# The inverse of the 16x16 diagonal blocks in a DeltaNet layer: VectorE's instructions given to GpSimd

## The chip, the cores and the metric

The kernel runs on 1 core of a Trainium2 chip. The metric is the device time of one execution in microseconds (us). In the profile the engines are PE (TensorE matmul), PEld (TensorE's weight loads), DVE (VectorE), ACT (ScalarE), POOL (GpSimd) and SP (SyncE, whose queue issues the DMAs here).

## The reference, cut to what matters

One layer of a streaming encoder: an input projection of 2176 tokens feeds three head groups (band attention, a gated DeltaNet, an S5 state space model), whose outputs go through an output projection and a feed-forward network. The change is in the DeltaNet. It works on chunks of 64 tokens and solves a unit lower triangular system in each:

```python
a_low = jnp.where(strict, jnp.einsum('bhnid,bhnjd->bhnij', k_beta, k) * decay, 0.0)
rhs = jnp.concatenate([v * beta[..., None], k_beta * jnp.exp(gc)[..., None]], axis=-1)
sol = lax.linalg.triangular_solve(a_low + jnp.eye(CHUNK, dtype=jnp.float32), rhs,
                                  left_side=True, lower=True, unit_diagonal=True)
u, w = sol[..., :d_v], sol[..., d_v:]
...
def step(state, xs):
    q_c, k_c, u_c, w_c, qk_c, gt_c = xs
    v_new = u_c - jnp.einsum('bhcd,bhde->bhce', w_c, state)
    o_c = jnp.einsum('bhcd,bhde->bhce', q_c, state) + jnp.einsum('bhij,bhje->bhie', qk_c, v_new)
    state = state * gt_c[..., None, None] + jnp.einsum('bhcd,bhce->bhde', k_c, v_new)
    return state, o_c
```

## The kernel before, in words

The mix stage runs three streams at once. The input projection (`project1`, then `project2_all`) is the dense one: each product is three fp32r matmuls (`mm3`, L63 to L67), whose operands are split into a high part by ACT (L60) and a low part by DVE (L61). The DeltaNet (`deltanet`, L166) goes over the 17 tiles of 128 tokens, in the order 0, 2, ..., 10, 16, 12, 14 of pairs (tile 16, the running streams, alone). The S5 stream joins when `project1` has ended. `mix` (L131) and `merge` (L121) interleave the three by hand-set paces; the Tile planner then lays the instructions out on each engine's queue at build time, and each engine runs its queue in that order.

For a pair of tiles the DeltaNet does this:

- `b_pre` (L474): convolution and SiLU (ACT L510, DVE L512, ACT L514, DVE L515), the norms (DVE L532 and the small ones of `rsqrt`, L343 to L350), factors `F` (DVE L544 to L549), the scaled q and k (DVE `qkn` L572 and `kdec` L577, POOL `qdkb` L574 and `R` L575, POOL `DM` L570), their transposes on PE (L583, L587), the products (PE L601) and their decays (DVE L603). The matrix `at` goes to DRAM and its 16x16 diagonal blocks come back as `blk` (SP L605, L606), one block on each partition: 32 partitions for a tile, 64 for a pair.
- `b_inverse` (L612): the changed function, once for a pair, 9 times in all. `Ti` begins as the identity (L620). Then 15 steps of forward substitution, each one product `tp` (L625) and one subtraction in `Ti` (L627), of 15 to 64 elements for a partition, each needing the one before it; then a transposed copy (L628). SP writes the two halves of `Ti` to the diagonal of a zeroed matrix in DRAM (`tD`, L635) and loads it back as `TU` (L636).
- `b_solve` (L640) on PE, DVE and ACT: products with `T` and `U` out of `TU` (PE L649), subtractions (DVE L661).
- `b_rec` (L674): the recurrence over the two chunks of a tile (PE L686 to L694, DVE L687 and L699, ACT L702), and `b_out` (L762): POOL `osq` L770, DVE L772, L775, L788, PE L786.

GpSimd has in this stage 7 instructions for a tile of the DeltaNet or less (L570, L574, L575, L608, L770, a few copies and memsets) and, from 600 us on, S5's products `tz` and `tw` (L957, L961). `Ti` has one buffer and `tp` too; `blk` has two, `TU` three.

Of the kernel before, what the change touches and what calls it, by code (L numbers as in the profile page):

```python
# [14 lines left out]
OP = mybir.AluOpType  # L15
# [26 lines left out]
class K:  # L42
# [292 lines left out]
    def rsqrt(self, pool, x, n, tag):  # L335

        V = self.nc.vector
        t = pool.tile([128, n], I32, name=tag + "t", tag=tag + "t")
# [3 lines left out]
        z = pool.tile([128, n], F32, name=tag + "z", tag=tag + "z")  # L342
        V.tensor_scalar(t, x.bitcast(I32), 1, None, OP.logical_shift_right)  # L343
        V.tensor_scalar(y, t, -1.0, float(0x5f3759df), OP.mult, OP.add)
        V.tensor_scalar(xh, x, -0.5, None, OP.mult)
        cur = y.bitcast(F32)
        for _ in range(3):
            V.tensor_tensor(s, cur, cur, OP.mult)
            V.tensor_tensor(s, s, xh, OP.mult)
            V.scalar_tensor_tensor(z, s, 1.5, cur, OP.add, OP.mult)  # L350
# [261 lines left out]
    def b_inverse(self, st, blk):  # L612

        nc = self.nc
        V = nc.vector
        bw = self.bw
        P = len(st) * 32
        Ti = bw.tile([P, 2, 16, 16], F32, name="Ti", tag="Ti", bufs=1)
        tp = bw.tile([P, 256], F32, name="tp", tag="tp")
        V.tensor_copy(Ti[:, 0], self.id16[:P])  # L620
        for j in range(15):
            m = 15 - j
            sh = [P, m, j + 1]
            pr = tp[:, :m * (j + 1)].rearrange("p (a b) -> p a b", a=m)
            V.tensor_tensor(pr, blk[:, j, j + 1:16].unsqueeze(2).to_broadcast(sh),  # L625
                            Ti[:, 0, j:j + 1, 0:j + 1].to_broadcast(sh), OP.mult)
            V.tensor_tensor(Ti[:, 0, j + 1:16, 0:j + 1], Ti[:, 0, j + 1:16, 0:j + 1], pr, OP.subtract)  # L627
        V.tensor_copy(Ti[:, 1], Ti[:, 0].rearrange("p i j -> p j i"))  # L628

        def load():  # L630
            for i, s in enumerate(st):
                k = s["t"] % NDIAG
                TU = bw.tile([128, 2, 4, 128], F32, name="TU", tag="TU", bufs=3)
                for u in range(2):
                    nc.sync.dma_start(self.diag_ap(self.tD[u, k]), Ti[i * 32:(i + 1) * 32, u])  # L635
                    nc.sync.dma_start(TU[:, u], self.heads_ap(self.tD[u, k]))  # L636
                yield TU[:, 0], TU[:, 1]
        return load
# [1296 lines left out]
```

## Time and profile before

| | before |
|---|---|
| median of 3 runs | 2851.4 us (2848.71 to 2852.71) |
| the profiled execution's own time | 2849.91 us |
| its span, first to last instruction | 2848.1 us |
| busy: PE, DVE, ACT, POOL | 2738.6, 1945.4, 1305.6, 1032.7 us |
| mean granted TensorE clock | 0.991 |

A row of the trace has the line of the kernel, the engine, what is written and read (`out<-in`, by the program's names) and the shape. Durations are in ns where a row gives min/median/max, otherwise in us. A wait row names who waited, for whom, the total in us, how many times, and the longest one. An engine's idle time matters where that engine sets the time.

### The profile page before, as it was taken

Reading aid. Unit: us, or ns where it says so; the run is one execution under the profiler, and the core shown is the slowest. Engines: PE = TensorE matmul, PEld = TensorE weight load, DVE = VectorE, ACT = ScalarE, POOL = GpSimd, SP = SyncE. Lnnn points to the kernel's source line nnn. Section 1 sums busy time; section 2 is a strip of 40 time slices with the busy share of each in tenths; the row PEclk is TensorE's granted clock in tenths of the full one; section 3 lists DMA queues with packets and bytes.
Section 4 is the critical chain, followed back from the end, with each engine's and each line's share of the span. In section 5 each row is a group of like instructions: output and inputs, shape, how many; then the busy total and the mean of one; then the engine's idle time right before and its main releaser. Section 6 shows DMA issues by size and latency. Waiting matters only on the chain.

```text
span 2848.1 us, 46357 instructions
## 1 busy us (share of the span) xinstructions
PE 2738.6 (96%) x16685; PEld 2405.1 (84%) x16685; DVE 1945.4 (68%) x4949; ACT 1305.6 (46%) x2714; POOL 1032.7 (36%) x914
## 2 busy tenths in 40 slices
PE   8999999989989899999999999999999999999998
PEld 8988888867677677788898998989989988999997
DVE  7587888788653788879855555576556557576766
ACT  3554554343355778612243443355334435444443
POOL 0010111232221232013354445345544453666664
PEclk9999999989999999999999999999999999999999
DMA  5644445555447652145631221153222214432321
GB/s 185 204 111 120 111 114 125 150 147 155 146 138 247 213 167 61 55 169 198 224 124 60 74 75 59 60 196 131 88 74 86 93 67 148 163 98 95 119 96 46
DMA packets 293436, 355.55 MB, mean 125 GB/s; under 512 B 85698, under 2 KB 218646, under 8 KB 292886
## 3 DMA queue, kind: packets, MB, share of 16 engines
q1 hardware_dynamic: 293206, 352.59, 39.4%
q8 instruction: 131, 2.15, 0.3%
q14 instruction: 99, 0.81, 0.1%
HBM read 280.25 MB, written 74.89 MB: 125 GB/s over the span
## 4 chain that ended last, share of the span: by engine, by line
PE 68%; DVE 16%; DMA 6%; issue 4%; ACT 3%; POOL 2%; SPq 1%; DVEq 0%; ACTq 0%; POOLq 0%
PE fdp L66 8%; PE fdp L65 8%; PE fdp L67 8%; PE pps L66 2%; PE pps L67 2%; PE pps L65 2%; PE fupz L67 2%; PE fupv L67 2%; PE fupv L65 2%; PE fupv L66 2%; PE fupz L65 2%; PE fupz L66 2%; PE fupx L65 2%; PE fupx L67 2%; PE fupx L66 2%
## 5 line engine op out<-in xcount | busy, mean ns | idle before, releaser
L1570 POOL TENSOR_TENSOR wu<-wur,wu 128x512 fp32r<-128x512 f32 x308 | 416.7, 1357 | 528.1 <-ACT wu L1569 527.4
L1696 DVE TENSOR_TENSOR fy<-fy,fdp 128x512 f32<-128x512 f32 x500 | 340.9, 685 | 255.8 <-PE fdp L67 255.5
L65 PE MATMUL fdp<-wdh,hh 128*128 128x512 f32 x1020 | 397.8, 390 | 1.2 <-DVE fy L1696 1.1
L66 PE MATMUL fdp<-wdl,hh 128*128 128x512 f32 x1020 | 397.3, 390 | 0.1
L67 PE MATMUL fdp<-wdh,hl 128*128 128x512 f32 x1020 | 397.1, 389 | 0.0
L1569 ACT CAST wu<-wur 128x512 fp32r<-128x512 f32 x308 | 189.6, 617 | 414.1 <-DMA wur<-in_w_upL 168.6
L65 PE MATMUL pps<-xh,wh 128*128 128x384 f32 (+2 forms) x800 | 279.6, 351 | 10.5 <-ACT xh L60 9.5
L66 PE MATMUL pps<-xl,wh 128*128 128x384 f32 (+2 forms) x800 | 279.3, 349 | 2.4 <-DVE xl L61 2.3
L67 PE MATMUL pps<-xh,wl 128*128 128x384 f32 (+2 forms) x800 | 277.1, 347 | 0.7 <-DVE wl L61 0.7
L65 PEld LDWEIGHTS fdp<-wdh,hh 128*128 128x128 f32 x1020 | 191.4, 188 | 41.0 <-DVE fy L1696 2.9
L67 PEld LDWEIGHTS fdp<-wdh,hl 128*128 128x128 f32 x1020 | 191.5, 188 | 40.0
L66 PEld LDWEIGHTS fdp<-wdl,hh 128*128 128x128 f32 x1020 | 191.5, 188 | 38.5 <-DVE wdl L61 0.7
L1643 DVE TENSOR_TENSOR hl<-fre,hh 128x384 fp32r<-128x384 f32 (+1 forms) x180 | 143.4, 797 | 85.1 <-ACT hh L1642 84.4
L60 ACT CAST wdh<-wdr 128x1024 fp32r<-128x1024 f32 x94 | 98.8, 1051 | 205.6 <-PE fdp L67 205.2
L65 PEld LDWEIGHTS pps<-xh,wh 128*128 128x128 f32 x800 | 151.9, 190 | 23.3 <-ACT xh L60 11.3
L61 DVE TENSOR_TENSOR wl<-wr,wh 128x512 fp32r<-128x512 f32 (+1 forms) x152 | 107.5, 716 | 86.3 <-ACT wh L60 84.2
L66 PEld LDWEIGHTS pps<-xl,wh 128*128 128x128 f32 x800 | 151.8, 190 | 14.3 <-DVE xl L61 5.5
L67 PEld LDWEIGHTS pps<-xh,wl 128*128 128x128 f32 x800 | 151.5, 189 | 12.4 <-DVE wl L61 2.5
L61 DVE TENSOR_TENSOR wdl<-wdr,wdh 128x1024 fp32r<-128x1024 f32 x94 | 133.1, 1421 | 6.6 <-ACT wdh L60 6.6
L60 ACT CAST wh<-wr 128x512 fp32r<-128x512 f32 (+1 forms) x152 | 92.3, 618 | 79.9 <-DMA wr<-in_w_inA 41.4
L1638 ACT ACTIVATE fre<-fre,ld_b_up 128x384 f32<-128x384 f32 (+1 forms) x144 | 85.9, 597 | 63.3 <-DVE fre L1647 40.3
L1229 ACT ACTIVATE P<-P,st 128x640 f32<-128x640 f32 (+4 forms) x128 | 97.2, 760 | 30.2 <-DVE st L1226 29.6
(569 smaller groups left out, 7241.7 us busy)
## 6 DMA issues: line engine op xcount, KB each, us to landing
wdr<-in_w_dnL SPq DMA_DIRECT2D x96, 512.0 KB
wur<-in_w_upL SPq DMA_DIRECT2D x88, 512.0 KB
wr<-in_w_inA SPq DMA_DIRECT2D x70, 512.0 KB
TU<-tD SPq DMA_DIRECT2D x34, 256.0 KB
y<-in_x SPq DMA_DIRECT2D x17, 512.0 KB
x<-y SPq DMA_DIRECT2D x17, 512.0 KB
fxr<-x SPq DMA_DIRECT2D x17, 512.0 KB
fy<-x SPq DMA_DIRECT2D x17, 512.0 KB
```

The costliest lines, as they stand in the source:

```text
L60: nc.scalar.copy(hi, src)
L61: nc.vector.tensor_tensor(lo, src, hi.bitcast(F32), OP.subtract)
L65: mm(out, lh, rh, start=first, stop=False, **kw)
L66: mm(out, lh, rl, start=False, stop=False, **kw)
L67: mm(out, ll, rh, start=False, stop=last, **kw)
L1229: self.nc.scalar.activation(x, x, AF.Exp, scale=-1.0, bias=st[:, q:q + 1], accum_out=st[:, 2 + q:3 + q])
L1569: self.nc.scalar.copy(hi, src)
L1570: P.tensor_tensor(lo, src, hi.bitcast(F32), OP.subtract)
L1638: nc.scalar.activation(r, src, AF.Relu, bias=self.bu[:, c * 2 + i:c * 2 + i + 1])
L1643: V.tensor_tensor(hl, r, hh.bitcast(F32), OP.subtract)
L1696: V.tensor_tensor(y, y, ps[x], OP.add)
```

## The change

`b_inverse` issues its 32 instructions (the identity copy, 15 products, 15 subtractions, the transposed copy) on GpSimd in place of VectorE. Shapes, tiles, buffers and the DMAs behind them stay as they are. `b_inverse` runs 9 times, so 288 instructions change their engine.

```diff
     def b_inverse(self, st, blk):
 
         nc = self.nc
-        V = nc.vector
+        P_ = nc.gpsimd
         bw = self.bw
         P = len(st) * 32
         Ti = bw.tile([P, 2, 16, 16], F32, name="Ti", tag="Ti", bufs=1)
         tp = bw.tile([P, 256], F32, name="tp", tag="tp")
-        V.tensor_copy(Ti[:, 0], self.id16[:P])
+        P_.tensor_copy(Ti[:, 0], self.id16[:P])
         for j in range(15):
             m = 15 - j
             sh = [P, m, j + 1]
             pr = tp[:, :m * (j + 1)].rearrange("p (a b) -> p a b", a=m)
-            V.tensor_tensor(pr, blk[:, j, j + 1:16].unsqueeze(2).to_broadcast(sh),
+            P_.tensor_tensor(pr, blk[:, j, j + 1:16].unsqueeze(2).to_broadcast(sh),
                             Ti[:, 0, j:j + 1, 0:j + 1].to_broadcast(sh), OP.mult)
-            V.tensor_tensor(Ti[:, 0, j + 1:16, 0:j + 1], Ti[:, 0, j + 1:16, 0:j + 1], pr, OP.subtract)
-        V.tensor_copy(Ti[:, 1], Ti[:, 0].rearrange("p i j -> p j i"))
+            P_.tensor_tensor(Ti[:, 0, j + 1:16, 0:j + 1], Ti[:, 0, j + 1:16, 0:j + 1], pr, OP.subtract)
+        P_.tensor_copy(Ti[:, 1], Ti[:, 0].rearrange("p i j -> p j i"))
```

## Rows read from the trace of the kernel before

**Rows 1.** Busy time by stretch: us, PE, PEld, DVE, ACT, POOL busy, PEclk, DMA share, GB/s.
```profile
165.00:700.00 535.00, 507.00 (x3761) 439.08 (x3760) 441.63 (x1706) 243.46 (x613) 106.60 (x165) 0.98 0.47 128
...
600.00:640.00 40.00, 31.20 (x167) 24.18 (x167) 37.44 (x120) 18.72 (x42) 15.48 (x19) 0.80 0.69 194
```

**Rows 2.** Instructions on the projection's PSUM tile: duration min/median/max, first and last start.
```profile
L67 PE MATMUL pps<-xh,wl x800: 274/338/628, 9.7 to 919.4; 128*128 128x384 f32 x91, 128*128 128x512 f32 x38, 128*128 128x256 f32 x31
```

**Rows 3.** What PE waited for, 165 to 700 us: total, times, longest.
```profile
PE bps L535 <- DVE s L515: 5.2, 3, 4.3
PE bps L587 <- POOL qdkb L574: 4.0, 7, 2.0
...
PE bqs L649 <- DMA TU<-tD: 0.4, 1, 0.4
...
PE brs L690 <- DVE vn L687: 0.3, 1, 0.3
```

**Rows 4.** Instructions on the tile Ti: by line, then their busy time from 165 to 760 us.
```profile
L625 DVE TENSOR_TENSOR tp<-blk,Ti x135: 155/200/701, 165.2 to 698.3; 64x15 f32<-64x15 f32 x16, 64x28 f32<-64x28 f32 x16, 64x39 f32<-64x39 f32 x16, 64x48 f32<-64x48 f32 x16
...
L628 DVE COPY Ti<-Ti x9: 367/371/1228, 172.6 to 699.8; 64x256 f32<-64x256 f32 x8, 32x256 f32<-32x256 f32 x1
...
sum 595.00, DVE 65.67; mean DVE 9.38
```

**Rows 5.** VectorE in order of time: start us, us; first and last of two inverses.
```profile
165.17 0.17 DVE L625 TENSOR_TENSOR tp<-blk,Ti 64x15 f32<-64x15 f32 x1 [2.31 <-DMA blk<-aD]
...
172.63 0.37 DVE L628 COPY Ti<-Ti 64x256 f32<-64x256 f32 x1
...
477.32 0.17 DVE L625 TENSOR_TENSOR tp<-blk,Ti 64x15 f32<-64x15 f32 x1
...
495.43 0.38 DVE L628 COPY Ti<-Ti 64x256 f32<-64x256 f32 x1
```

**Rows 6.** GpSimd's instructions of lines L570 and L574: duration ns min/median/max.
```profile
L570 POOL TENSOR_TENSOR DM<-DT,ld_c_mtri x17: 723/737/1354, 142.7 to 629.1; 128x256 f32<-128x256 f32 x17
...
L574 POOL TENSOR_TENSOR qdkb<-qk,F x17: 1037/1432/2250, 140.1 to 667.8; 128x512 f32<-128x512 f32 x17
```

**Rows 7.** GpSimd in order of time, feed-forward stage: two instructions, the second needs the first.
```profile
2572.57 1.29 POOL L1576 TENSOR_TENSOR wur<-wur 128x512 f32<-128x512 f32 x1
2573.94 1.30 POOL L1577 TENSOR_TENSOR wur<-wur 128x512 f32<-128x512 f32 x1
```

**Rows 8.** VectorE, then GpSimd, in order of time, 184 to 187 us; GpSimd at 621 us.
```profile
184.23 0.15 DVE L549 TENSOR_TENSOR F<-F,b_kd 128x4 f32<-128x4 f32 x1
184.31 0.68 DVE L572 TENSOR_TENSOR qkn<-qk,F 128x512 f32<-128x512 f32 x1
184.91 1.00 DVE L548 TENSOR_TENSOR F<-F,b_egc 128x4 f32<-128x4 f32 x1
...
184.46 1.43 POOL L574 TENSOR_TENSOR qdkb<-qk,F 128x512 f32<-128x512 f32 x1 [14.48 <-ACT s L510]
...
621.51 2.48 POOL L575 TENSOR_TENSOR R<-qk,F 128x256 f32<-128x256 f32 x1 [1.45 <-DVE F L549]
```

**Rows 9.** VectorE's groups, 165 to 700 us: busy us, mean ns, idle before.
```profile
L512 DVE SCALAR_TENSOR_TENSOR s<-cin,ld_b_cw,s 128x128 f32<-128x128 f32 x234 | 80.2, 358 | 1.9 <-ACT s L510 1.4
L61 DVE TENSOR_TENSOR wl<-wr,wh 128x512 fp32r<-128x512 f32 (+1 forms) x71 | 49.6, 701 | 3.7 <-ACT wh L60 3.4
```

**Rows 10.** The chain that ended last, 170 to 190 us: start us, us.
```profile
174.63 3.22 DMA TU<-tD
177.90 1.10 PE bqs L649 x8
```

**Rows 11.** SP's and PE's instructions in order of time, around 500 us.
```profile
497.43 2.08 SPq L636 DMA_DIRECT2D TU<-tD  x4
...
502.65 1.00 PE L649 MATMUL bqs<-at,TU 128*128 128x64 f32 x8
```

**Rows 12.** What SP's queue waited for, 165 to 705 us: total, times, longest.
```profile
SPq L635 <- DVE Ti L627: 7.3, 3, 4.5
```

## The prediction

> **What bounds the kernel now.** I read the busy times by stretch first, to find where the changed instructions lie and which engine is full there. They lie between 165 and 700 us, and in those 535 us PE is busy for 507.0 and DVE for 441.6, or 83% [rows 1]. The projections' matmuls run until 919 us [rows 2], far past the last inverse, so PE is the filler and the bound: whatever happens to an inverse counts only as far as PE idles longer or less. PE's idle time in the stretch is 535 - 507 = 28 us. The list of PE's waits says who ended it: fourteen of its rows name DVE, from 5.2 us down to 0.3, and they add up to 19.5 us; one names POOL with 4.0; one, of 0.4 us, names the load of `TU`, the way by which an inverse reaches PE [rows 3]. From 600 to 640 us DVE is busy for 37.4 of 40 us, PE for 31.2, and the granted clock is 0.80 (so part of that time passes at 1.2 GHz instead of 2.4) after PE has idled for 4.3 us on DVE's L515 [rows 1, 3]. So the stage is bound by PE, and what holds PE up is mostly DVE.
>
> Second I read the inverse itself. Its 288 instructions keep DVE busy for 65.7 us in all [rows 4]. As a chain, the first takes from 165.17 to 173.00 us, 7.8 us; the sixth from 477.32 to 495.81, 18.5 us, since DVE does other work between its links [rows 5].
>
> **Part one: what DVE gets back.** 65.7 us of work leave it. Some comes back as waiting, because the two engines hold each other up. DVE's L548, 128x4, took 1.00 us, where its sister L549 took 0.15: it ended with POOL's L574, which itself took 1.43 us against 1.04 at best, having started just behind DVE's L572 [rows 6, 8]. And a POOL instruction of 128x256, for which 0.73 us is usual, took 2.48 us at 621 us while DVE was full [rows 6, 8]. The Trainium skill, "SBUF — State Buffer", section "Who interferes with whom", says of this that a VectorE instruction with two SBUF inputs and a GpSimd instruction that reads SBUF exclude each other, and the later one waits for the whole of the earlier; the trace agrees (1.00 us against 0.15), and by that rule the change moves work between two engines of which one often stands still.
>
> How much comes back: between nothing and the whole time that the chain executes on POOL, 76 us (9 x 8.5, below). The two groups of DVE that read two SBUF operands in the rows shown, L512 and L61 with `wl`, are 80.2 + 49.6 = 130 of the 441.6 - 65.7 = 376 us that stay [rows 1, 9]; with the smaller ones I call it half, so about 35 us. Net relief: 65.7 - 35, about 30 us, 7% of DVE's time in the stretch. PE's waits on DVE (19.5 us) should fall by more than 7%, as they gather where DVE is full; I take a third, **-7 us**. Bounds: 0, and -28 (all 19.5 us and the 8 us that a clock of 0.80 costs in 40 us).
>
> **Part two: the chain on POOL.** No row shows POOL with 64 partitions and 15 to 64 elements. Its nearest rows are 737 ns for 256 elements [rows 6] and 1290 ns for 512 [rows 7]: 2.16 ns an element on top of 184 ns. The 30 linked instructions have 2 x 680 = 1360 elements together, so 30 x 0.184 + 1360 x 0.00216 = 8.5 us of execution. A link costs 0.08 us between two dependent instructions (2572.57 + 1.29 to 2573.94) [rows 7], 2.4 us for 30. The transposed copy of 256 elements lies between DVE's 0.37 [rows 4] and the 0.74 of a POOL instruction of that size; I take 0.5. Undisturbed chain: 11.4 us. Below, if small instructions cost only their share of 0.737 us: 6.8. Above, if each cost as much as 256 elements: 25. The identity copy is no link; it runs ahead, and counts as cheap as now.
>
> On top comes the wait for DVE, once for each link: 0.01 us by L570 (median less minimum), 0.40 by L574, which DVE's L572 always meets [rows 6]. I take 0.15, as links become ready at any moment, like L570: 30 x 0.15 = 4.5 us. Chain with waits: about 16 us, against 8 to 18 on DVE. So the latency hardly changes; what changes is whether the fixed order of the queues expects it.
>
> That order puts PE's first product with `TU` close behind its landing: the load issued at 174.63 lands after 3.22 us, and PE starts at 177.90, with nothing in between [rows 10]. Around 500 us a load issued at 497.43 should land by some 500.8, and PE starts at 502.65, 1.8 us of slack [rows 11]. Mean slack: 1 us. If the planner counts the undisturbed chain, each inverse comes 4.5 - 1 = 3.5 us too late, 9 x 3.5 = 31 us. Behind PE's waiting product stand the projections' matmuls, which have to be late with it. But while PE stands, DVE and ACT run ahead and later waits shrink, so I take half: **+15 us**. Bounds: 0 (the planner expects the waits, or PE is late anyway) and 55 (twice the waits for each link, nothing made up: 9 x (9 - 1) = 72, less what PE regains from DVE).
>
> **Part three: the queues it is moved past.** On DVE the inverse no longer delays the norm, split and recurrence work, which is in part one. On POOL it stands before `qdkb`, `R`, `DM` and `osq`, for each tile. `qdkb` feeds PE's transposes, which waited 4.0 us for it, 7 times [rows 3]. One link lasts some 0.3 us, so a neatly woven queue adds little; a late chain adds its lateness. **+1 us**, bounds 0 and 9. The first link waits for the landing of `blk`, on POOL as it did on DVE (2.31 us at 165.17) [rows 5]; POOL's queue stands behind it, and POOL is busy for 106.6 of 535 us [rows 1], so little is lost. SP's write of `Ti` waited 7.3 us for DVE's last links, 3 times, up to 4.5 [rows 12]; with weight loads queued behind it, a late chain there costs as it did. The number and sizes of the DMAs stay, at no cost: they are issued by SP either way. Memory stays, too.
>
> **Sum.** -7 + 15 + 1 = +9 us on a span of 2848.1 us. The profiled execution took 2849.9 us, 1.8 more than its span, and lies 1.5 us under the median of the runs, so I carry +9 to the median: 2851.4 + 9 = **2860 us**. About 0.2%, 5.7 us, is what a measurement of this kernel tells from no change.
>
> **The rivals.**
>
> *DVE's relief wins (faster).* Mechanism: DVE is what PE waits for, 19.5 of 28 us, and the 600 to 640 us stretch loses clock besides [rows 1, 3]. If half of those waits (10 us) and half of the clock's price (4) go and late chains cost 2 us, it is 12 us faster: 2839. For it: on DVE the chain took up to 18.5 us, on POOL it may be shorter. Against: the half that comes back as waiting. It decides if chains on POOL stay under what the order allows, slack of 1 us included.
>
> *No change, within 4 us: 2851.* Both parts are small because PE is full for 95% of the stretch. The Trainium skill, "Perfetto Trace Analysis", section "Optimizing Scalar/DVE Operations", points this way: offloading between those two engines might not help, as they share a read port. No row here weighs the sum of that.
>
> *POOL is starved (much slower).* Each time a link ends, DVE's next instruction with two operands takes its turn first, 0.36 us for L512, 0.70 for L61 [rows 9], as the 2.48 us of L575 show in the extreme [rows 8]. With 0.4 us a link, 12 us an inverse, 11 beyond the slack; half made up, 9 x 5.5 = 50 us; with the relief gone too, less 10 that stalled DVE work would have cost: +40, 2891. Against: L570's median lies only 0.01 us over its minimum.
>
> That the change would not do what it says can be left out: the engine is named in each call.
>
> **How the numbers follow.** Forecast (late chains cost more than the relief, +2 to +18 us): 0.37. DVE's relief wins: 0.27. No change: 0.22. Starved: 0.14. A quarter of the forecast's case and little of the faster one's fall within 5.7 us: slower 0.37 x 0.75 + 0.14 = 0.42, same 0.22 + 0.09 + 0.01 = 0.32, faster 0.26. The range runs from 2837 (under the faster case's 2839) to 2888 (just short of the starved case), which leaves out about a tenth on either side. Signs are mixed, so the forecast's own range is 2853 to 2869.
>
> **What would show it.** Right: 288 instructions move; DVE's busy time from 165 to 700 us falls by 30 us or so, not 66, with L512 and L61 longer in the mean; a chain on POOL takes 14 to 18 us; PE's waits for `TU` grow from 0.4 us to 10 and more, those on DVE fall below 15. Wrong: chains of 11 to 12 us and PE's waits for `TU` still under 3 us (then faster or the same), or chains over 22 us (then starved). What would upset the whole sum is a new order of the queues that moves PE's idle time to somewhere the rows above don't show.

## The result, and the profile after

The changed kernel takes 2920.1 us (median of 4 runs, 2917.3 to 2923.4), the kernel before 2850.7 us beside it: 1.0249 times as long, 95% interval 1.0237 to 1.0262. That is 69 us slower, where 2860 us and a range of 2837 to 2888 had been forecast. The sign was right, the size was not.

Almost all of the loss lies in the mix stage. The last matmuls of the projection start at 990.8 us, 71 us later than before [rows 2]; the span grew by 73.5 us, from 2848.1 to 2921.6. In the busy times by stretch (us of the stretch, then PE, PEld, DVE, ACT, POOL busy, PEclk, DMA share, GB/s), the first row answers to [rows 1]; the second takes the stage to its end:

```profile
165.00:700.00 535.00, 470.48 (x3367) 412.29 (x3365) 357.91 (x1275) 226.07 (x575) 174.38 (x398) 0.92 0.42 113
...
165.00:991.00 826.00, 728.90 (x4819) 619.66 (x4818) 524.97 (x1685) 344.02 (x811) 241.74 (x498) 0.93 0.47 131
```

The same stretch of the kernel before, to the end of its projection:

```profile
165.00:919.70 754.70, 706.92 (x4816) 599.40 (x4815) 555.24 (x1972) 342.80 (x811) 148.56 (x211) 0.98 0.50 143
```

With the same matmuls (4816 and 4819 records), PE stands idle for 826.0 - 728.9 = 97.1 us in place of 47.8, and is busy for 728.9 us in place of 706.9. So 49 of the 71 us are idle time. The other 22 are longer matmuls, which go with the lower granted clock (0.93 for 0.98).

The instructions on the tile `Ti` (duration ns min/median/max, first and last start) answer to [rows 4], now on POOL:

```profile
L625 POOL TENSOR_TENSOR tp<-blk,Ti x135: 203/282/1192, 166.2 to 748.6; 64x15 f32<-64x15 f32 x16, 64x28 f32<-64x28 f32 x16, 64x39 f32<-64x39 f32 x16, 64x48 f32<-64x48 f32 x16
L627 POOL TENSOR_TENSOR Ti<-Ti,tp x135: 212/294/769, 166.5 to 748.9; 64x15 f32<-64x15 f32 x16, 64x28 f32<-64x28 f32 x16, 64x39 f32<-64x39 f32 x16, 64x48 f32<-64x48 f32 x16
...
L628 POOL COPY Ti<-Ti x9: 594/603/676, 178.4 to 749.2; 64x256 f32<-64x256 f32 x8, 32x256 f32<-32x256 f32 x1
```

From the first link to the end of the copy, the nine chains take 11.8 to 15.4 us, 13.6 in the mean; on DVE they took 7.8 to 22.9, 15.5 in the mean. So the chains did not get longer, and yet the work that needs them is late. What PE waited for (165 to 770 us: total, times, longest) answers to [rows 3]:

```profile
PE bqs L649 <- DMA TU<-tD: 28.2, 6, 7.6
PE s5p L1019 <- DMA Tm<-kS: 10.5, 1, 10.5
PE brs L786 <- DVE osq L775: 8.0, 7, 2.4
PE pps L65 <- ACT wh L60: 6.2, 1, 6.2
PE bps L587 <- POOL qdkb L574: 5.6, 7, 2.4
PE pps L67 <- DVE wl L61: 5.3, 1, 5.3
```

SP's queue over the same time, which answers to [rows 12]:

```profile
SPq L635 <- POOL Ti L627: 77.7, 9, 11.8
```

SP now comes to the write of `Ti` too early at every inverse, by 77.7 / 9 = 8.6 us; before, 3 times and by 4.5 us at most [rows 12]. So the planner's order has SP at the write some 5 us after the first link of a chain that takes 13.6. What duration the planner reckons with, no run shows. PE comes too early as well. Here is PE in order of time at the first inverse, with the idle time before an instruction in brackets:

```profile
175.72 0.33 PE L66 MATMUL pps<-xl,wh 128*128 128x384 f32 x1
183.69 1.97 PE L649 MATMUL bqs<-at,TU 128*128 128x64 f32 x8 [7.63 <-DMA TU<-tD]
```

PE has nothing left before its first product 9.9 us after the first link (175.72 + 0.33 - 166.2). Before, it arrived there 12.3 us after the link, waited 0.4 us for `TU` [rows 3] and started at 12.7 us (165.17 [rows 5] to 177.90 [rows 10]). Counted so for all nine inverses, PE arrives 16.4 us after the first link in the mean, where it was 22.0. The chain needs 13.6, and from its last copy to PE's product at least another 4.7 us pass (179.01 to 183.69). PE's order thus leaves the chain 5.2 us at the first inverse and 11.7 in the mean.

What it costs that SP stands is seen at the last inverse. SP in order of time:

```profile
737.68 0.42 SPq L210 DMA_DIRECT2D wr<-in_w_inA  x1
749.15 0.98 SPq L635 DMA_DIRECT2D tD<-Ti  x2
750.22 1.36 SPq L983 DMA_DIRECT2D Tm<-kS  x2
```

and PE, which needs that `Tm` for the S5 stream, not for the DeltaNet:

```profile
753.56 0.79 PE L1019 MATMUL s5p<-U,Tm 128*128 128x136 f32 x2 [10.53 <-DMA Tm<-kS]
```

From 738.1 to 749.15 us SP issued nothing; the load of `Tm` stood behind the write.

### The profile page after: what moved, and what is told of

It reads as the page before. It is cut to its first block, busy times and chain, and to the rows that moved or that the text cites. A ratio compares the mean times of both kernels' runs of the same rounds, so it can differ in the third digit from the quotient of the medians.

```text
span 2921.6 us, 46374 instructions
## 1 busy us (share of the span) xinstructions
PE 2760.6 (94%) x16685; PEld 2424.7 (83%) x16685; DVE 1913.3 (65%) x4661; ACT 1307.0 (45%) x2714; POOL 1128.8 (39%) x1202
## 4 chain that ended last, share of the span: by engine, by line
PE 67%; DVE 13%; DMA 7%; POOL 4%; issue 4%; ACT 3%; SPq 1%; DVEq 0%; ACTq 0%; POOLq 0%
PE fdp L66 8%; PE fdp L65 8%; PE fdp L67 8%; PE pps L67 3%; PE pps L66 3%; PE pps L65 3%; PE bqs L649 2%; PE fupv L65 2%; PE fupv L67 2%; PE fupv L66 2%; PE fupz L65 2%; PE fupz L67 2%; PE fupz L66 2%; PE fupx L65 2%; PE fupx L67 2%
## 5 line engine op out<-in xcount | busy, mean ns | idle before, releaser
L60 ACT CAST wh<-wr 128x512 fp32r<-128x512 f32 (+1 forms) x152 | 92.7, 619 | 97.1 <-PE pps L66 40.7
```

Source lines behind the costliest of these rows:

```text
L60: nc.scalar.copy(hi, src)
```

## The experiments

**Three theories.** Theory 1, the order: the queues of PE and SP are laid out for a chain much shorter than the real one, so both stand. Theory 2, the port: the chain on POOL and DVE's work hold each other up. Theory 3, POOL's queue: what stands behind the chain on POOL is late. Where the expectations speak of holding a queue, every instruction of the mix on the named engine is tied to its predecessor in a given list, by place in the queue alone, without a semaphore; the planner lays out the rest. All ratios are against the kernel before, run on the same chip.

**1. The change in the old order.** PE's and SP's queues as they stand in the kernel before.

```diff
+ORDER = {
+...
+}
+
+def hold_order(nc, tc):
+    byname = {i.name: i for i in nc.cur_bb.bb.instructions}
+...
     with tile.TileContext(nc) as tc:
         K(nc, tc, A).run()
+        hold_order(nc, tc)
```

> The changed kernel, with the instructions of TensorE's and SyncE's queues held, up to the end of the mix, in the order that they have in the kernel before (PE and SP alone; DVE, ACT and POOL are left to the planner). Theory 1 (the order: the planner counts the POOL chain some 8 us too short and moves the solves' products and the tD writes ahead, so PE and SP stand before they are ready): in the old order PE comes to the first product 12 to 33 us after the first link and the POOL chain with its DMAs needs about 18, so only the first two or three inverses are late, by 4 to 6 us each; against that stands DVE's relief: 2840 to 2865 us, PE's waits for TU under 15 us in all (28.2 in the changed kernel), SP's waits for the chain under 25 (77.7). Theory 2 (POOL's chain holds DVE and POOL at the shared port) and theory 3 (POOL's own queue is held up by the chain, and what waits behind it is late): the order is no matter, 2900 us or more.

2877.0 us, 1.0091 (1.0076 to 1.0106): 44 of the 69 us are gone, and 25 stay, more than theory 1 alone allows. PE's and SP's waits, 165 to 770 us, and DVE's on POOL:

```profile
PE pps L66 <- DVE xl L61: 10.8, 2, 10.6
PE bqs L649 <- DMA TU<-tD: 8.8, 3, 5.9
```

```profile
SPq L635 <- POOL Ti L627: 12.4, 2, 9.9
```

```profile
DVE WB L964 <- POOL tw L961: 13.5, 4, 8.9
DVE ms L772 <- POOL osq L770: 11.3, 11, 3.8
```

The time lies above theory 1's range and below the other theories'. The waits for `TU` and for `Ti` are small again, as expected. New is that DVE stands for POOL. POOL in order of time at the longest of these waits (a chain had begun at 628.0 us, and nothing but its links ran until `tw`):

```profile
639.47 0.23 POOL L625 TENSOR_TENSOR tp<-blk,Ti 64x28 f32<-64x28 f32 x1
639.66 0.63 POOL L961 TENSOR_TENSOR tw<-st,pis 128x256 f32<-128x256 f32 x1
640.26 0.23 POOL L627 TENSOR_TENSOR Ti<-Ti,tp 64x28 f32<-64x28 f32 x1
640.46 0.63 POOL L961 TENSOR_TENSOR tw<-st,pis 128x256 f32<-128x256 f32 x1
```

and DVE, which needs the second `tw`:

```profile
641.12 0.69 DVE L964 TENSOR_TENSOR WB<-WB,tw 128x512 f32<-128x512 f32 x1 [8.90 <-POOL tw L961]
```

PE's wait of 10.6 us for `xl` follows from it, as `xl` stands behind `WB` in DVE's queue. Since PE's order is the same in both kernels, one of its instructions can be set beside the other: PE falls back by 6.6 us up to the first product with `TU`, and by 9.5 us in one step at 645.5 us.

**2. The old kernel in the new order.** The reverse: the chain on DVE, PE and SP held as in the changed kernel. The edit is the one of experiment 1, on the kernel before, with the changed kernel's list.

> The kernel before, its chain on DVE, with TensorE's and SyncE's queues held in the order of the changed kernel. Theory 1: the loss comes with the order, without any POOL chain: PE stands at TU and SP at the tD write as in the changed kernel, 2880 to 2930 us, PE's waits for TU 20 us or more. Theories 2 and 3: nothing runs on POOL that did not before, 2845 to 2860 us.

2928.6 us, 1.0265 (1.0248 to 1.0282). With the inverse on DVE and nothing new on POOL, the order by itself costs 77 us. That is more than the change itself lost: on DVE the seventh and the eighth chain take 21.4 us each here, and PE stands 10.7 and 11.6 us for them. PE and SP wait in the places where they wait in the changed kernel, though the engine behind them is another:

```profile
PE bqs L649 <- DMA TU<-tD: 40.6, 8, 11.6
PE s5p L1019 <- DMA Tm<-kS: 11.2, 2, 10.6
PE brs L786 <- DVE osq L775: 6.9, 6, 1.5
PE pps L65 <- ACT wh L60: 6.1, 1, 6.1
```

```profile
SPq L635 <- DVE Ti L627: 53.9, 7, 13.7
```

**3. No chain, old order.** What DVE's relief is worth.

```diff
-        tp = bw.tile([P, 256], F32, name="tp", tag="tp")
-        P_.tensor_copy(Ti[:, 0], self.id16[:P])
-        for j in range(15):
-...
-        P_.tensor_copy(Ti[:, 1], Ti[:, 0].rearrange("p i j -> p j i"))
+        for u in range(2):
+            nc.vector.scalar_tensor_tensor(Ti[:, u], blk, 0.0, self.id16[:P], OP.mult, OP.add)
```

> The changed kernel without a chain at all (two DVE instructions write the unit matrix into Ti from blk, the inverse is left out), TensorE's and SyncE's queues in the order of the kernel before: what DVE's relief alone is worth in that order. Working of the prediction: 65.7 us off DVE are worth at most 28 us: 2823 to 2845 us. If 2848 to 2853, DVE's relief is worth nothing in that order and there was never anything to gain but by the order. Theories 2 and 3 say the same of this run as theory 1.

2850.2 us, 0.9993 (0.9984 to 1.0002): nothing. 18 instructions stand where 288 stood, and nothing is won. The first stretch [rows 1]:

```profile
165.00:700.00 535.00, 508.11 (x3777) 441.36 (x3776) 412.82 (x1446) 244.77 (x614) 108.45 (x166) 0.99 0.48 129
```

DVE is busy for 29 us less than the 441.6 of [rows 1], and PE for 1 us more. PE's waits on DVE, 19.5 us in [rows 3], still add up to 19.2 us. One of them had named the inverse (first row, kernel before); without it PE waits for `osq` (second row, this run; lines behind `b_inverse` are 8 lower):

```profile
PE brs L786 <- DVE Ti L627: 2.7, 3, 1.5
```

```profile
PE brs L778 <- DVE osq L767: 5.1, 6, 2.1
```

**4. POOL's load alone.** The kernel before, with the links a second time on POOL, into a scratch tile.

```diff
         V.tensor_copy(Ti[:, 1], Ti[:, 0].rearrange("p i j -> p j i"))
+        G = nc.gpsimd
+        Tz = bw.tile([P, 1, 16, 16], F32, name="Tz", tag="Tz", bufs=1)
+        tz = bw.tile([P, 64], F32, name="tz", tag="tz", bufs=1)
+        G.tensor_copy(Tz[:, 0], self.id16[:P])
+        for j in range(15):
+...
+            G.tensor_tensor(pr, blk[:, j, j + 1:16].unsqueeze(2).to_broadcast(sh),
+                            Tz[:, 0, j:j + 1, 0:j + 1].to_broadcast(sh), OP.mult)
+            G.tensor_tensor(Tz[:, 0, j + 1:16, 0:j + 1], Tz[:, 0, j + 1:16, 0:j + 1], pr, OP.subtract)
```

> The kernel before, and beside its DVE chain the same links (without the last copy) on POOL into a scratch tile that nobody reads: POOL's load without anybody waiting for it and without DVE's relief. Theory 1: little, 2850 to 2870 us. Theory 2 (contention at the shared port) and theory 3 (POOL's queue held up): most of the 69 us loss, 2890 us or more.

2888.7 us, 1.0122 (1.0106 to 1.0139): 37 us, between the two answers. Nobody uses what POOL computes here, and the kernel is slower all the same. But no queue is held, and PE's instructions stand in another order than in the kernel before, so part of the 37 us can be order; and two chains run at the same moment. Experiment 5 is the cleaner one.

**5. POOL's load, DVE relieved, old order.** The change in the old order, its chain into a scratch tile; the solve gets the unit matrix as in experiment 3.

```diff
+        Tz = bw.tile([P, 2, 16, 16], F32, name="Tz", tag="Tz", bufs=1)
-        P_.tensor_copy(Ti[:, 0], self.id16[:P])
+        P_.tensor_copy(Tz[:, 0], self.id16[:P])
...
+        for u in range(2):
+            nc.vector.scalar_tensor_tensor(Ti[:, u], blk, 0.0, self.id16[:P], OP.mult, OP.add)
```

> The kernel with the old order held (PE and SP), but nobody waits for the chain: the whole chain still runs on POOL, into a tile that nobody reads, and two DVE instructions write the unit matrix into Ti (the inverse is left out of the result). What is left of the 25 us over the kernel before is POOL's load alone. Theory 3 (POOL's queue: DVE and PE stand for tw, osq, qdkb that are queued behind the chain; in the run with the old order DVE stood 8.9 us for tw, and TensorE fell back 9.5 us there): the first late product (8 us with its clock) goes, the rest stays: 2862 to 2872 us. If the chain's lateness is all of it: 2848 to 2856 us.

2876.3 us, 1.0085 (1.0068 to 1.0102): a miss, above both ranges. Nobody waits for the chain, and yet 26 us are lost, as many as the 25 of experiment 1. So the late inverse is not needed for them. That the two losses are equal is partly chance: the late first product was 6.6 us of experiment 1's, and here other waits for POOL are longer. PE's waits, then DVE's on POOL (lines from `b_inverse` on are 3 higher here: L773 is `osq`, L964 `tw`):

```profile
PE bps L587 <- POOL qdkb L574: 12.6, 4, 11.9
PE brs L789 <- DVE osq L778: 9.0, 6, 3.9
```

```profile
DVE ms L775 <- POOL osq L773: 13.0, 11, 4.8
DVE WB L967 <- POOL tw L964: 4.8, 3, 3.6
```

Set beside experiment 3 in the same PE order, PE falls back in steps of 3.0, 3.6, 11.9 and 2.8 us; the first two are transposes that wait for `osq`, the third one that waits for `qdkb`. At the third, PE in order of time and POOL behind the chain (the last copy of the chain is `Tz<-Tz`):

```profile
645.67 0.69 PE L587 MATMUL bps<-ld_c_ident,qdkb 128*128 128x128 f32 x2 [11.90 <-POOL qdkb L574]
```

```profile
642.24 0.59 POOL L629 COPY Tz<-Tz 64x256 f32<-64x256 f32 x1
...
643.39 1.23 POOL L964 TENSOR_TENSOR tw<-st,pis 128x256 f32<-128x256 f32 x2
644.58 1.03 POOL L574 TENSOR_TENSOR qdkb<-qk,F 128x512 f32<-128x512 f32 x1
```

**6. The same links at another place in POOL's queue.** Experiment 5, with POOL's other work held in its old order and the links put into the stretches in which POOL stood idle in the trace of the kernel before. The edit is a third list in `ORDER`.

> The kernel in which nobody waits for POOL's chain, PE and SP in the old order (2876 us, 26 above the kernel before), and now POOL's queue held too: POOL's other work in the order of the kernel before, and the 32 links of each chain put where POOL stood idle in the trace of the kernel before (at most as many links in a gap as fit it). The same links, the same port time; only their place in POOL's queue is another. Theory 3 (tw, osq and qdkb wait in POOL's queue behind the chain): 2848 to 2860 us. Theory 2 (the shared port): nothing is won, 2868 us or more.

2860.4 us, 1.0032 (1.0021 to 1.0043). That is the upper edge of theory 3's range. The links are the same 288 instructions, and 16 of the 26 us are gone by another place in POOL's queue, as theory 3 has it. The big waits are gone with them:

```profile
PE brs L789 <- DVE osq L778: 5.4, 7, 2.1
PE bps L587 <- POOL qdkb L574: 2.9, 7, 1.7
```

Some 10 us stay. The durations of DVE's instructions outside the inverse (the same 1685 in each run, from 165 us to the end of the projection) add up to 617.5 us here, 606.0 in experiment 3 and 607.2 in experiment 5. So the links make DVE's other work 11.5 us longer where they are spread over POOL's idle time, and 1.2 us longer where they run as a block. The 11.5 us fit the port, theory 2; that they make the 10 us is argued, not shown. If they do, the place in POOL's queue is worth more than the 16 us.

**7. POOL's other work on DVE.** The change in the old order, with seven lines of POOL's work in the mix put on DVE.

```diff
-            nc.gpsimd.tensor_tensor(as8(qdkb), qk[:, i], fb(2, 8), OP.mult)
+            nc.vector.tensor_tensor(as8(qdkb), qk[:, i], fb(2, 8), OP.mult)
...
-        nc.gpsimd.tensor_tensor(sq, of, of, OP.mult)
+        nc.vector.tensor_tensor(sq, of, of, OP.mult)
```

> The changed kernel with the old order of PE and SP held, and seven lines of POOL's other work in the mix put on DVE (DM, qdkb, R, at, osq, tz, tw), so that nothing but small copies stands behind the chain on POOL; DVE gets about 48 us of it back for the 65.7 that it gave. Theory 3 (POOL's queue): the loss by work queued behind the chain goes, only the first late inverse stays: 2852 to 2863 us. Theory 2 (the shared port): the chain still takes its port time, and DVE has more to do in it: 2872 us or more.

2885.3 us, 1.0124 (1.0109 to 1.0140): a miss for theory 3. It lies in theory 2's range, but does not decide for theory 2 either. The waits for `qdkb`, `osq` and `tw` on POOL are gone, and others have come: PE stood for `TU` for 10.5 us, up to 9.1 at a time, and the lines on DVE now wait on DVE's queue, where they hold up what is behind them. Experiment 6, which moves nothing between engines, is the cleaner one.

**8. No chain, nothing held.** The kernel of experiment 3 in the planner's own order.

> The changed kernel without any chain (two DVE instructions write the unit matrix into Ti), nothing held: the planner's own order for a chain that takes no time. The bound of what any cheaper or better placed chain could give. With the old order the same kernel ran in the time of the kernel before; if the order for a short chain is as good as the old one, 2840 to 2852 us; if taking PE to the solves earlier costs something by itself, above 2855 us.

2849.9 us, 1.0000 (0.9990 to 1.0009). If the inverse took no time at all and the queues were laid out for that, the kernel would be no faster. PE comes to the solves early here, 7.4 us after the first write of `Ti` in the mean, where it was 18.3 in experiment 3. That costs nothing in itself; it costs where the inverse isn't there yet.

**9. One queue held at a time.** The change with PE's queue alone in the old order, then SP's alone; the edits are experiment 1's with one list each.

> The changed kernel with TensorE's queue alone held in the old order; SP's is the planner's for the chain on POOL. Tells the two queues apart: if PE's order carries the 44 us that the old order gave back, 2873 to 2885 us; if SP's early tD writes, with the loads queued behind them, carry half of it, about 2895 to 2905 us.

> The changed kernel with SyncE's queue alone held in the old order, TensorE's left to the planner. With PE's alone held it took 2913 us, with both 2877. If SP's early tD writes carry the loss of the order (the loads of weights, cin and Tm stand behind them), 2872 to 2890 us; if the two orders cost only together, 2895 us or more.

PE alone: 2913.0 us, 1.0220 (1.0195 to 1.0246). SP alone: 2887.7 us, 1.0128 (1.0109 to 1.0148). The first is a miss, above both of its ranges. With PE's queue held, PE's waits for `TU` are small, and 63 us are lost all the same, 36 more than with SP held too. What is left is SP's new order, in which it comes early to the writes:

```profile
PE bqs L649 <- DMA TU<-tD: 6.0, 2, 5.3
```

```profile
SPq L635 <- POOL Ti L627: 56.9, 8, 9.4
```

With SP's queue held, the planner put most of PE's products late by itself (PE arrives 29.5, 29.1 and 27.4 us after the first link at the fourth to sixth inverse, where in the changed kernel it was 17.4, 21.9 and 13.8). So the 32 us that the second run gives back aren't SP's share alone.

**10. Another queue for the write and the load.** The change, nothing held, the two DMAs on ScalarE's queue, then on GpSimd's (the diff of the first).

```diff
-                    nc.sync.dma_start(self.diag_ap(self.tD[u, k]), Ti[i * 32:(i + 1) * 32, u])
-                    nc.sync.dma_start(TU[:, u], self.heads_ap(self.tD[u, k]))
+                    nc.scalar.dma_start(self.diag_ap(self.tD[u, k]), Ti[i * 32:(i + 1) * 32, u])
+                    nc.scalar.dma_start(TU[:, u], self.heads_ap(self.tD[u, k]))
```

> The changed kernel, nothing held, with the writes of Ti to tD and the loads of TU issued by ScalarE instead of SyncE (two words of two lines). SP's queue then never stands for the chain. If SP's blocked loads carry the loss of the order (32 of 43 us by the runs that hold one queue), 2875 to 2895 us, unless ScalarE's own work, now behind the same wait, gives it back: then 2900 us or more, with ScalarE's queue standing for Ti where SP's stood.

> The same with GpSimd issuing the writes and loads: they stand right behind the chain on its own queue, so nobody waits for the chain but the solve; POOL then stands for each write to land before it issues the load. If SP's blocked loads carry the loss: 2870 to 2895 us. If POOL's longer standing costs more than SP's did: above 2900 us, with qdkb, osq and tw later.

2934.6 us, 1.0312 (1.0297 to 1.0327), and 2943.0 us, 1.0340 (1.0322 to 1.0357): both worse than the change. PE's wait for `TU`, on ScalarE's queue and on GpSimd's:

```profile
PE bqs L649 <- DMA TU<-tD: 45.5, 7, 9.8
```

```profile
PE bqs L649 <- DMA TU<-tD: 62.4, 8, 10.7
```

SP no longer stands for `Ti`, but on ScalarE's queue the standing has only moved. ACT in order of time at the first inverse:

```profile
169.87 0.22 ACT L420 ACTIVATE b_beta<-ba 128x24 f32<-128x24 f32 x1 [0.80 <-DMA ba<-baS]
175.84 2.05 ACTq L635 DMA_DIRECT2D tD<-Ti  x4
```

At its nine writes ACT stands for `Ti` for 61 us in all, up to 11.7 at a time, and its other work stands behind them. On GpSimd's queue POOL stands for the landing of the writes (13.3 us, 12 times), and PE waits longer for `TU` than in any other run. So neither run takes PE's early arrival by itself. The held queues show less than that: SP's new order alone, with PE in the old one, keeps most of the loss (63 us), and both in the old order give back 44 of 69. How the order's loss divides between PE and SP stays open.

**11. All three queues held.** The change, its result used, with PE's and SP's queues in the old order and the links in POOL's old idle stretches.

> The whole change, its result used, with three queues held: PE's and SP's in the old order, and POOL's other work in the old order with the links put into POOL's idle stretches of the kernel before (for the last three inverses partly as one block, since POOL's later work there waits for the solve). If the loss is order (43 us) plus place in POOL's queue (16 us) plus about 10 us for the chain wherever it stands, this takes 2858 to 2868 us, with some 6 us of wait for TU at the first inverse in it. If the late inverse and the queue's place are not two things, so that awaiting the chain costs again what the place gave back: 2872 us or more.

2891.5 us, 1.0161 (1.0144 to 1.0178): a miss, 47 us above the kernel before. With POOL's other work between its links a chain takes 17.7 us in the mean (11.3 to 22.2), and PE stands for it again:

```profile
PE bqs L649 <- DMA TU<-tD: 31.2, 6, 9.9
```

So the terms don't add for a chain that is awaited. Two places on POOL were tried: in one the chain goes first and `qdkb`, `osq` and `tw` are late (experiment 1, 25 us), in the other they go first and the chain is late (47 us).

## Why the prediction was wrong

**What bounds the kernel.** That PE is the bound and fills the stage held. That it is held up mostly by DVE, and so gains when DVE is relieved, did not. Nor does the low clock from 600 to 640 us follow from the 4.3 us that PE idled on L515: in the trace of the kernel before the granted clock stood at 0.50 from 599.2 to 609.4 us, and that wait lay within, from 601.1 to 605.4.

**Part one, -7 us.** Its lower end, 0, was the truth: experiments 3 and 8 take the whole chain away and win nothing, within 0.2%. DVE's busy time over the whole program did fall from 1945.4 to 1913.3 us, the 30 us or so that were forecast, but not since the rest came back as waiting for POOL. With no chain anywhere (experiment 3) it falls to 1915.2 us, and 7 of these are the two new instructions for each inverse. The 65.7 us of [rows 4] are the durations of the inverse's instructions, and they overlap the records of DVE's other work: in the trace of the kernel before DVE is busy with the inverse alone for 40.6 of them. And the step from a freer DVE to a shorter wait of PE failed: PE's waits on DVE, which were to fall by a third from 19.5 us, are 22.5 in the changed kernel over the same stretch and 19.2 without any chain. The Trainium skill, "Perfetto Trace Analysis", section "Optimizing Scalar/DVE Operations", says that moving work between these two engines may not help, as they share a port; the outcome agrees, but the reason that runs here show is another: there was nothing to win by DVE.

**Part two, the chain.** 16 us were forecast, 13.6 measured; the links' price (0.184 us and 2.16 ns an element, 0.28 us for a link of mean size) met the medians of 282 and 294 ns. Of the 4.5 us for waits for DVE at most 2.2 came (13.6 - 11.4).

**Part two, the lateness: the step that failed.** "If the planner counts the undisturbed chain, each inverse comes 4.5 - 1 = 3.5 us too late, 9 x 3.5 = 31 us", and then "I take half: +15 us". The step took the old order, with its slack of 1 us [rows 10, 11], as given, and asked only how late the chain comes in it. In its place the runs showed a new order, which has SP at the write some 5 us after the first link of a chain of 13.6 us: SP was 8.6 us early at each of nine inverses, and PE stood for `TU` for 28.2 us in all. In the old order the change is only 25 us slower (experiment 1), since PE comes to all inverses but the first 17 us or more after the first link; the new order, with the chain on DVE where it had been, costs 77 (experiment 2). That the 31 us before the halving lie near these 28.2 is luck, as they were worked out from waits for DVE in the old order. The halving had no ground either: PE's idle time grew by 49 us, more than by these waits, and the lower clock, for which this part had no term, made it 22 us more. The last sentence of the prediction named a new order of the queues as what would upset the sum; it should have been a rival with a price.

**Part three, +1 us.** Both halves were too small. For SP, "a late chain there costs as it did": it waited for 77.7 us in place of 7.3 [rows 12], and its new order alone, with PE in the old one, makes some 36 us (2913.0 - 2877.0). For POOL, "a late chain adds its lateness", with an upper end of 9 us: POOL's queue costs 16 (experiments 5 and 6) with nobody waiting for the chain.

**The rivals.** POOL starved (2891 us) came nearest in size and was wrong in its mechanism: the links ran at their undisturbed price. It was the other way round: POOL's chain starved others. DVE's relief wins is ruled out by experiments 3 and 8. No change is ruled out by the result, though for DVE's part alone it was right.

**What stays open.** How the 10 us that are left in experiment 6 come about; what duration the planner reckons with; and how the order's loss divides between PE and SP, as a kernel with PE in the new order and SP in the old was not tried.

## What to carry to other kernels

Before work is moved off an engine, take it away altogether and time that: here one such run would have shown that there was nothing to gain. Where a planner lays out the queues at build time, a move between engines can change the order of all of them; ask how much time the new order leaves the moved work, and what stands behind each instruction that waits for it, on DMA-issuing queues above all. A queue that is mostly idle (POOL, busy for 20% here) is not free for a chain of 14 us if someone waits for the other instructions on it.

## What was not expected of the hardware

The clock made the stalls dearer. At the first inverse of the changed kernel the granted clock stood at its upper level (1.00, 2.4 GHz) up to 178.5 us, where PE had been idle since 176.05, and at the lower one (0.50, 1.2 GHz) from 178.7 to 188.9 us. Busy times by stretch:

```profile
170.00:178.50 8.50, 6.05 (x35) 5.74 (x33) 5.05 (x16) 5.14 (x13) 7.10 (x21) 1.00 0.11 31
178.70:188.90 10.20, 5.21 (x24) 5.14 (x25) 0.01 (x1) 2.31 (x5) 0.70 (x2) 0.50 0.77 213
190.00:200.00 10.00, 9.99 (x72) 8.88 (x71) 9.74 (x43) 6.03 (x14) 2.15 (x2) 1.00 0.20 62
```

In that spell the eight products with `TU` took 1.97 us, where the same eight had taken 1.10 us [rows 10]. Over the stage the same matmuls kept PE busy for 22 us longer.

The two engines hindered each other less than two rows of before had suggested [rows 8]. With the 288 links as a block (experiment 5) DVE's other instructions were 1.2 us longer in all, and 11.5 us with the links spread over POOL's idle time (experiment 6), 2% of their 606 us, where 35 had been put down to it. The Trainium skill, "SBUF — State Buffer", section "Who interferes with whom", has a VectorE instruction with two SBUF inputs and a GpSimd instruction that reads SBUF exclude each other. Single instructions show it here [rows 8]; how much of the time it decides stays open, 10 us at most in experiment 6.
